# A batched matmul with a decaying running sum: one group of slots by seven block products, and a planner's order in place of a written one

## The chip, the cores and the metric

The kernel runs on one core of a Trainium2 chip. The metric is the device time of one execution in microseconds (us). Before the change the median of three runs is 904.89 us (904.84 to 904.93).

The core's engines work side by side and meet only through semaphores: TensorE (PE) multiplies matrices and writes its results to PSUM; VectorE (DVE), ScalarE (ACT) and GpSimd (POOL) work on tiles; SyncE (SP) issues transfers here. Each engine takes its instructions strictly in the order in which the program issued them, so an instruction that waits holds up all that stand behind it on its engine.

## The reference

```python
# x: 16 x 2048 x 1024, w: 1024 x 1024, decay: 1024, all float32
xw = x @ w
out[:, 0, :] = xw[:, 0, :]
for t in range(1, S):
    out[:, t, :] = decay * out[:, t - 1, :] + xw[:, t, :]
```

One matmul of 32768 x 1024 by 1024 x 1024, and behind it a recurrence over 2048 time steps in each of the 16 x 1024 columns.

## The kernel before

**Tiling.** Time is cut into 64 chunks of 512 steps (four per batch entry). Two neighbouring chunks of one batch entry form a group; the last two chunks are handled singly. The 1024 output columns are eight blocks of 128 (n = 0 to 7), the 1024 inputs eight blocks (k = 0 to 7). A *slot* is one group and one n: 16 matmuls (L131) of 128x128 by 128x512 in bf16, eight for each half of a PSUM tile ps of 128 x 1024. There are three such tiles, used in turn, and single-bank tiles spare and spare1. 31 groups have eight slots each, the last two chunks eight shorter ones each: 264 slots. Slots 112 to 119 are group 14, the first half of a batch entry.

**Input.** `load` (L101) brings a quarter of a chunk into xb (three buffers) by a transfer on POOL's queue that casts to bf16. `turn` (L109) transposes blocks on DVE into xw (two buffers; row L115). `part` (L119) separates the two interleaved bf16 halves on ACT into xt (five buffers; row L123), two instructions for a chunk, named X and Y in the agenda. xt is what the matmuls stream.

**Recurrence.** In a slot's result the columns are on the partitions and time lies along the row, so that a scan on DVE does the recurrence. A tile is either *unpaired*: one full scan over 1024 steps straight from PSUM (`run`, L228); or *paired*: ACT copies ps to xs (`copy`, L185) and scales its even steps by the decay (`odd`, through `decayed`, L170), POOL adds these to the odd steps (`join`, L205), DVE scans the 512 odd steps with the squared decay (`scan`, L210), ACT scales the result (`even`, L170) and POOL adds it to the even steps (`fill`, L253). `zero` (L199, L201) sets the first element of the result tile so, `save` (L257) keeps the last column in keep for the next group of the batch entry. Three of four tiles are paired. Here so has four buffers, xs three, h four.

**Output.** `back` (L265) transposes so on DVE into ot (four buffers). When four slots, a *lump* of 2 MB, are in ot, `Outlet.store` (L289) issues four transfers of 512 KB on SP, one per quarter of the partitions. The first `back` of a later lump that takes the same buffer waits for their landing.

**Order.** What is issued when is written out by hand: `agenda` lists, for the first 34 slots and the last 20, the deeds by letter (p copy, g odd, z zero, j join, S scan, h even, c fill, k save, B back, T turn, X and Y part, L load). In between `usual` makes the same list for each slot, with turns and parts due a fixed number of slots ahead (`later`) and one or two loads per slot. `perform` carries a list out.

Of the kernel before, what the change touches and what calls it, by code (L numbers as in the profile page):

```python
# [2 lines left out]

# [6 lines left out]
FP32 = mybir.dt.float32  # L10
# [15 lines left out]
def kernel(  # L26
# [26 lines left out]
    nc = tc.nc  # L53
# [12 lines left out]
    R = K // 2  # L66
    CH = D // 2
    CR = CH // NQ

    const = ctx.enter_context(tc.tile_pool(name="const", bufs=1))  # L70
    sb = ctx.enter_context(tc.tile_pool(name="sb", bufs=1))
# [20 lines left out]
    wcols = wsb.rearrange("p k (h r) q i -> p k h q r i", h=2)  # L92

    def ot_tile(nj):
        return ring(sb, "ot", 4, [128, nj, CR])

    xb_of = {}
    xw_of = {}
# [19 lines left out]

    def part(c, copy, m0, m1, j0=0, j1=NJ):  # L119
        if c not in xt_of:  # L120
            xt_of[c] = ring(sb, "xt", 5, [128, M, 2, TL], BF16)
        src = xw_of[c][:, m0:m1, j0:j1].rearrange("p m j i e -> p m e (j i)")
        pin(copy(out=xt_of[c][:, m0:m1, :, j0 * P:j1 * P], in_=src))  # L123

# [16 lines left out]
    class Tile:  # L141
# [3 lines left out]
        def __init__(self, g, n, ps, outlets):  # L145
            self.b, self.t0 = chunks[g[0]]
            self.T = TL * len(g)
            self.n, self.ps, self.outlets = n, ps, outlets
            self.paired = n % R != R - 1
            if len(tiles) in flips or len(tiles) - len(slots) in flips:  # L150
                self.paired = not self.paired
            self.turn = len(tiles)
            self.lot = sum(t.paired for t in tiles)
            self.prev = None if self.t0 == 0 else last[n]
            if self.t0 + self.T < S:
                last[n] = const.tile([128, 1], FP32, name=f"keep{n}", bufs=2)
                self.keep = last[n]
            else:
                self.keep = None

        @property
        def so(self):
            if not hasattr(self, "held"):
                self.held = sb.tile([128, 2 * TL + 2], FP32, name=f"so{self.turn % 4}")
            return self.held

        def decayed(self, src, h=None):
            if h is None:
                h = ring(sb, "h", 4, [128, TL])[:, 0:self.T // 2]
            pin(nc.scalar.activation(  # L170
                out=h, in_=src, func=mybir.ActivationFunctionType.Copy,
                scale=dec[:, self.n:self.n + 1]))
            return h
# [5 lines left out]
                self.zero()  # L179
                self.join()  # L180

        def copy(self):
            self.xs = sb.tile([128, 2 * TL], FP32, name=f"xs{self.lot % 3}")[:, 0:self.T]
            for t, ps in self.parts():
                pin(nc.scalar.copy(out=self.xs[:, t:t + ps.shape[1]], in_=ps))  # L185

        def odd(self):
            self.g = ring(sb, "h", 4, [128, TL])[:, 0:self.T // 2]
            for t, ps in self.parts():
                size = ps.shape[1]  # L190
                self.decayed(ps[:, 0:size:2], self.g[:, t // 2:(t + size) // 2])

        def parts(self):
            some = self.ps if isinstance(self.ps, tuple) else (self.ps,)
            return [(i * self.T // len(some), ps) for i, ps in enumerate(some)]

        def zero(self):
            if self.prev is None:
                pin(nc.gpsimd.memset(self.so[:, 1:2], 0.0))  # L199
            else:  # L200
                pin(nc.scalar.copy(out=self.so[:, 1:2], in_=self.prev))  # L201

        def join(self):
            odds = self.xs[:, 1:self.T:2]
            pin(nc.gpsimd.tensor_tensor(out=odds, in0=self.g, in1=odds, op=ALU.add))  # L205

        def scan(self):
            T, n, so = self.T, self.n, self.so
            if self.paired:
                pin(nc.vector.tensor_tensor_scan(  # L210
                    out=so[:, 3:T + 2:2],
                    data0=squares[-1][:, n:n + 1].to_broadcast([128, T // 2]),
                    data1=self.xs[:, 1:T:2],
                    initial=0.0 if self.prev is None else self.prev,
                    op0=ALU.mult,
                    op1=ALU.add,
                ))
            else:
                for t, ps in self.parts():
                    self.run(ps, t, ps.shape[1])  # L220

        def run(self, ps, t, size):
            n, so = self.n, self.so
            if t:
                before = so[:, t + 1:t + 2]
            else:
                before = 0.0 if self.prev is None else self.prev
            pin(nc.vector.tensor_tensor_scan(  # L228
                out=so[:, t + 2:t + 2 + size],
                data0=dec[:, n:n + 1].to_broadcast([128, size]),  # L230
                data1=ps,
                initial=before,
                op0=ALU.mult,
                op1=ALU.add,
            ))
# [5 lines left out]
        def complete(self):  # L241
            if self.paired:
                self.even()
                self.fill()
            if self.keep is not None:
                self.save()

        def even(self):
            self.h = self.decayed(self.so[:, 1:self.T + 1:2])

        def fill(self):
            T = self.T
            pin(nc.gpsimd.tensor_tensor(  # L253
                out=self.so[:, 2:T + 2:2], in0=self.h, in1=self.xs[:, 0:T:2], op=ALU.add))

        def save(self):
            pin(nc.scalar.copy(out=self.keep, in_=self.so[:, self.T + 1:self.T + 2]))  # L257

        def back(self, half=None):
# [13 lines left out]
    class Outlet:  # L273


        def __init__(self, ns, nj, half=0, queues=(nc.sync,), pieces=1):
            self.pieces = pieces
            self.ns, self.missing, self.half = ns, set(ns), half
            self.nj, self.t0, self.queues = nj, half * nj * P, queues
            self.ot = ot_tile(nj)  # L280

        def store(self, b, t0):
            n0 = self.ns[0]
# [132 lines left out]
    def turn_and_load(c):  # L416
# [58 lines left out]
        18: "g16 T7 L h15 j16 p17 g17 B14 z17 c15 X7",  # L475
        19: "S16 j17 p18 B15 L g18 L S17 k16 h16 z18 j18",
        20: "Y7 S19 L c16 k17 h17 T8 k19 L c17",
        21: "p20 g20 L S18 X8 j20 B17 B19",
        22: "L h18 p21 c18 B16 k18 g21 B18 Y8 z20 L j21 S20",
        23: "p22 z21 z22 S21 L h20 g22 T9 c20 h21",  # L480
        24: "k21 k20 j22 S23 X9 L c21 Y9 B20 L",
        25: "B23 k23 p24 B21 g24 z24 j24 S22 z25",
        26: "p25 T10 k22 h22 g25 c22 S24 X10 j25",
        27: "B22 p26 S25 g26 z26 Y10 j26",
        28: "S27 h25 h24 c25 S26 c24",
        29: "B27 h26 c26 T11 p28 g28 j28 B24",
        30: "p29 B25 g29 z28 j29 S28 z29 S29",
        31: "h28 p30 c28 B26 g30 h29 B28 j30 z30",
        32: "c29 S31 S30 h30 B29 c30 p32 g32 z32 j32 B30 B31 L L",
        33: "p33 g33 z33 j33 S32 h32 c32 k32 L L",  # L490
        -20: "z-20",
        -19: "p-20 g-20",
        -18: "j-20 S-19 S-20 k-19 B-19",
# [16 lines left out]
        -1: "S-2 h-4 c-4 a-1 b-1 V",  # L510
    }
    flips = (1, 13, 15, -19, -18, -11, -8, -6, -3, -2)
    later = {}
    begun = {"T": 12, "X": 11, "Y": 11}
    for c in range(5, nch):
        first = c // 2 * K
        ahead = (7, 6, 4) if c % 2 else (11, 10, 8)
        for letter, a in zip("TXY", ahead):
            if c >= begun[letter]:
                later.setdefault(first - a, []).append(f"{letter}{c}")  # L520

    def usual(s):
        paired = [t.paired for t in tiles]
        do = [f"P{s}"] if paired[s] else []
        if paired[s - 1]:
            do.append(f"S{s - 1}")
        if not paired[s]:
            do.append(f"S{s}")
        do.append(f"C{s - 1}")
        if paired[s - 2]:  # L530
            do.append(f"B{s - 2}")
        if not paired[s - 1]:
            do.append(f"B{s - 1}")
        return do + later.get(s, []) + ["L"] * (2 if len(loads) > NQ else 1)

    def rest(s):
        do = [f"S{s - 1}"] if tiles[s - 1].paired else []
        do.append(f"C{s - 1}")
        if tiles[s - 2].paired:
            do.append(f"B{s - 2}")  # L540
        return do + [f"B{s - 1}"] + later.get(s, []) + ["L"] * len(loads)

    def perform(do):
        for deed in do:
            deeds[deed[0]](int(deed[1:] or 0))

    perform(agenda[-99].split())
    spares = [spare] + [ring(psp, "spare1", 1, [128, TL])]
    for step, (g, n) in enumerate(slots):
        T = TL * len(g)  # L550
        left = step - len(slots)
        if n % R == 0:
            ns, nj = range(n, n + R), T // P
            outlets = [Outlet(ns, nj)]
        if left == -R:
            outlets = []
        if step == 0:
# [48 lines left out]
            for k, l in todo:  # L606
                matmul(ps[:, l * TL:(l + 1) * TL], n, k, xt_of[g[l]])
        tiles.append(Tile(g, n, ps, outlets))
        do = agenda.get(step, agenda.get(left) if left >= -20 else None)
        if do is None:  # L610
            do = usual(step)
        else:
            do = do.split()
            if left == -20:
                do = rest(step) + do
        perform(do)
    assert not loads
# [1 line left out]
_INS = ['x', 'w', 'decay']  # L619
# [26 lines left out]
```

## Time and profile before

| what | value |
|---|---|
| median of three runs | 904.89 us |
| the profiled execution | 905.68 us, span 903.9 us, granted clock 0.999 |
| L131, matmuls into ps from xt, 128x512 | x3976, 859.0 us busy |
| L228, full scan of 128x1024 on DVE | 2260 ns, with a carried state 2321 ns |
| L210, paired scan of 128x512 on DVE | 1219 ns, with a carried state 1279 ns |
| L170, scaling of 512 steps on ACT | from so 775 ns, from ps 693 ns |
| DVE waited for L205 (POOL) | 50.9 us, 65 times, longest 1.3 us |
| stores landed, 140 to 200 us / 200 to 400 us (median) | 18.4 us / 11.7 us |
| loads landed, 140 to 200 us / 200 to 400 us (median) | 12.3 us / 7.6 us |

The span is the time between the first and the last event of the profiled execution; the execution's own time is a little longer. Busy times of one engine can overlap slightly at their edges. A row such as "L265 DVE STREAM_TRANSPOSE ot<-so" names the source line, the engine, the operation, and the tiles out and in; behind the bar stand the busy time in all, the mean of one in ns, and the idle time just before them with what ended it.

### The profile page before, as it was taken

Reading aid. Unit: us, or ns where it says so; the run is one execution under the profiler, and the core shown is the slowest. Engines: PE = TensorE matmul, PEld = TensorE weight load, DVE = VectorE, ACT = ScalarE, POOL = GpSimd, SP = SyncE. Lnnn points to the kernel's source line nnn. Section 1 sums busy time; section 2 is a strip of 40 time slices with the busy share of each in tenths; the row PEclk is TensorE's granted clock in tenths of the full one; section 3 lists DMA queues with packets and bytes.
Section 4 is the critical chain, followed back from the end, with each engine's and each line's share of the span. In section 5 each row is a group of like instructions: output and inputs, shape, how many; then the busy total and the mean of one; then the engine's idle time right before and its main releaser. Section 6 shows DMA issues by size and latency. Waiting matters only on the chain.

```text
span 903.9 us, 12113 instructions
## 1 busy us (share of the span) xinstructions
PE 896.4 (99%) x4217; PEld 412.7 (46%) x4217; DVE 825.5 (91%) x628; ACT 686.3 (76%) x957; POOL 656.7 (73%) x755
## 2 busy tenths in 40 slices
PE   8999999999999999999999999999999999999997
PEld 5544444444444444444444444444444444444444
DVE  4999998999999999999998999999999999999997
ACT  4899967777877877877778778778777787787742
POOL 7978678777767768677677677777777776776632
PEclk9999999999999999999999999999999999999999
DMA  9999999999999999999999999999999999999868
GB/s 186 190 215 215 226 256 217 215 237 236 254 242 260 243 251 257 248 237 226 224 237 229 224 229 229 230 224 229 231 227 228 233 232 222 226 233 211 176 143 235
DMA packets 402542, 204.77 MB, mean 227 GB/s; under 512 B 8752, under 2 KB 401456, under 8 KB 402480
## 3 DMA queue, kind: packets, MB, share of 16 engines
q1 hardware_dynamic: 265168, 134.76, 61.0%
q0 software_dynamic: 137024, 68.70, 56.6%
q8 instruction: 33, 0.54, 0.2%
q10 hardware_dynamic: 288, 0.52, 0.2%
q14 instruction: 29, 0.24, 0.1%
HBM read 138.42 MB, written 134.22 MB: 302 GB/s over the span
## 4 chain that ended last, share of the span: by engine, by line
PE 97%; DMA 1%; POOL 0%; issue 0%; DVE 0%; DVEq 0%; POOLq 0%
PE ps L131 96%; DMA xb<-in_x_dram 1%; PE spare L131 1%; POOL xb L105 0%; PE spare L395 0%; PE ps L395 0%; DVE h L399 0%; DVE xw L115 0%; DVEq L115 0%; POOLq L630 0%
## 5 line engine op out<-in xcount | busy, mean ns | idle before, releaser
L131 PE MATMUL ps<-xt,wsb 128*128 128x512 bf16 (+1 forms) x4028 | 866.3, 378 | 0.0
L131 PEld LDWEIGHTS <-wsb 128*128 128x128 bf16 x4168 | 407.5, 98 | 478.0 <-ACT wsb L313 0.8
L205 POOL TENSOR_TENSOR xs<-h,xs 128x512 f32<-128x512 f32 (+1 forms) x190 | 242.8, 1278 | 188.1 <-ACT h L170 85.3
L185 ACT COPY xs<-ps 128x1024 f32<-128x1024 f32 (+1 forms) x190 | 188.9, 994 | 152.9 <-PE ps L131 148.1
L265 DVE STREAM_TRANSPOSE ot<-so 128x1024 f32<-128x1024 f32 (+1 forms) x260 | 300.0, 1191 | 2.1 <-POOL so L199 1.1
L253 POOL TENSOR_TENSOR so<-h,xs 128x512 f32<-128x512 f32 (+1 forms) x190 | 241.0, 1270 | 43.7 <-ACT h L170 27.8
L123 ACT COPY xt<-xw 128x2048 bf16<-128x2048 bf16 (+3 forms) x136 | 242.3, 1790 | 8.7 <-DVE xw L115 8.7
L105 POOL DMA_DIRECT2D xb<-in_x_dram x264 | 174.0, 660 | 5.6 <-DMA xb<-in_x_dram 3.2
L170 ACT ACTIVATE h<-so,dec 128x512 f32<-128x512 f32 (+1 forms) x190 | 145.3, 766 | 28.7 <-DVE so L210 25.2
L115 DVE STREAM_TRANSPOSE xw<-xb 128x2048 f32<-128x2048 f32 (+3 forms) x78 | 147.4, 1901 | 8.0 <-DMA xb<-in_x_dram 7.9
L210 DVE TENSOR_TENSOR_SCAN so<-spare,keep,xs 128x512 f32<-128x512 f32 (+1 forms) x97 | 119.9, 1239 | 26.7 <-POOL xs L205 26.4
L210 DVE TENSOR_TENSOR_SCAN so<-spare,xs 128x512 f32<-128x512 f32 x93 | 113.3, 1219 | 27.4 <-POOL xs L205 24.5
L170 ACT ACTIVATE h<-ps,dec 128x512 f32<-128x512 f32 (+1 forms) x190 | 130.0, 684 | 0.0
L228 DVE TENSOR_TENSOR_SCAN so<-dec,ps 128x1024 f32<-128x1024 f32 x34 | 76.8, 2260 | 1.0 <-ACT h L170 1.0
L228 DVE TENSOR_TENSOR_SCAN so<-dec,keep,ps 128x1024 f32<-128x1024 f32 (+1 forms) x35 | 75.9, 2168 | 0.2 <-issue 0.2
L257 ACT COPY keep<-so 128x1 f32<-128x1 f32 x136 | 25.3, 188 | 9.5 <-DVE so L228 9.0
L201 ACT COPY so<-keep 128x1 f32<-128x1 f32 x97 | 18.4, 191 | 2.7 <-DVE ot L265 2.4
L131 PE MATMUL spare<-xt,wsb 128*128 128x512 bf16 (+3 forms) x60 | 12.6, 329 | 0.0
L131 PE MATMUL ps<-xw,wsb 128*128 128x256 bf16 (+3 forms) x68 | 11.2, 301 | 0.4 <-DVE xw L115 0.4
L199 POOL MEMSET so<- 128x1 f32 x93 | 10.7, 117 | 0.6 <-DVE ot L265 0.6
L331 PE MATMUL spare<-idle 128*128 128x512 bf16 x22 | 6.8, 479 | 1.2 <-DVE idle L321 1.2
L306 POOL DMA_DIRECT2D ot<-in_w_dram x12 | 6.6, 552 | 1.7 <-DMA xb<-in_x_dram 0.8
(39 smaller groups left out, 37.9 us busy)
## 6 DMA issues: line engine op xcount, KB each, us to landing
out_dram<-ot SPq DMA_DIRECT2D x248, 512.0 KB, 10.9
xb<-in_x_dram POOLq DMA_DIRECT2D x248, 256.0 KB, 7.9
out_dram<-ot SPq DMA_DIRECT2D x12, 256.0 KB, 4.2
ot<-in_w_dram POOLq DMA_DIRECT2D x12, 128.0 KB, 5.6
xb<-in_x_dram POOLq DMA_DIRECT2D x8, 128.0 KB, 5.4
out_dram<-xb SPq DMA_DIRECT2D x3, 256.0 KB
xb<-in_x_dram POOLq DMA_DIRECT2D x4, 144.0 KB, 7.0
ot<-in_w_dram ACTq DMA_DIRECT2D x2, 256.0 KB, 5.2
```

The source lines that it names most:

```text
L105: pin(nc.gpsimd.dma_start(out=xb_of[c][quad(q), j0:j1], in_=_ap(x, [[D, P], [P * D, j1 - j0], [1, CQ]], (b * S + t0 + j0 * P) * D + q * CQ)))
L115: pin(nc.vector.transpose(out=dst.rearrange("p (m j i) -> p j m i", m=M, i=P)[:, j0:j1, m0:m1], in_=src.rearrange("p (j m c) -> p j m c", ...
L123: pin(copy(out=xt_of[c][:, m0:m1, :, j0 * P:j1 * P], in_=src))
L131: pin(nc.tensor.matmul(out=ps[:, t0:t1] if ps.shape[1] >= t1 else ps, lhsT=lhs, rhs=rhs, start=(k == 0 and t0 == start), stop=(stop and k ...
L170: pin(nc.scalar.activation(out=h, in_=src, func=mybir.ActivationFunctionType.Copy, scale=dec[:, self.n:self.n + 1]))
L185: pin(nc.scalar.copy(out=self.xs[:, t:t + ps.shape[1]], in_=ps))
L205: pin(nc.gpsimd.tensor_tensor(out=odds, in0=self.g, in1=odds, op=ALU.add))
L210: pin(nc.vector.tensor_tensor_scan(out=so[:, 3:T + 2:2], data0=squares[-1][:, n:n + 1].to_broadcast([128, T // 2]), data1=self.xs[:, 1:T:2 ...
L228: pin(nc.vector.tensor_tensor_scan(out=so[:, t + 2:t + 2 + size], data0=dec[:, n:n + 1].to_broadcast([128, size]), data1=ps, initial=befor ...
L253: pin(nc.gpsimd.tensor_tensor(out=self.so[:, 2:T + 2:2], in0=self.h, in1=self.xs[:, 0:T:2], op=ALU.add))
L257: pin(nc.scalar.copy(out=self.keep, in_=self.so[:, self.T + 1:self.T + 2]))
L265: pin(nc.vector.transpose(out=outlet.ot[:, :, c0:c0 + P], in_=self.so[:, 2 + t0:2 + t0 + nj * P].rearrange("p (i t) -> p i t", t=P)))
```

## The change

The order of slots 34 to 243 is no longer written by hand. `steady` makes a list of jobs, each with an engine, an assumed cost, a key (about when it should start), and the jobs it waits for; `in_order` walks through them in assumed time and gives each engine, whenever it is free, the ready job with the smallest key; the program is then issued in that order. Each engine's start in that walk is `BEGUN`; a load is assumed to land after 11.0 us, a store after 13.0. Loads have a key and an earliest time of their own, evenly spaced. Turns are cut in two halves.

Group 14 (`merged`) computes its 2 x 2 blocks (two halves of the inputs; two chunks as columns; two blocks n of the weights) by seven products of four matmuls each instead of eight. For that, POOL forms 20 differences of weights (`wd`) from about 170 us before the group on, and three sums on DVE and one on POOL combine the group's parts (`sums`; the last is written over xt). The products go to two halves of a ps tile and a spare; partial results are lifted from PSUM by ACT (`lift`) and combined by DVE (`join` in `mixed_pair`). Between a lift or join and the next product in the same bank, PE waits.

Further: the copy of ps goes straight to so (xs is gone; so has seven buffers, ot three, xt four); a lump leaves in 16 transfers of 128 KB (`pieces=4`); which tiles are unpaired is chosen by `SHARE`, by the distance to group 14: none in it, fewer right behind it, a third in the group before, else a quarter. In the agenda of slots 20 to 33 some parts (X8 to Y10) are issued later and loads and last deeds are left to the plan. The names and lines of unchanged deeds stay; L265 becomes L276, L210 L221, L289 L305.

```diff
-            xt_of[c] = ring(sb, "xt", 5, [128, M, 2, TL], BF16)
+            xt_of[c] = ring(sb, "xt", XTS, [128, M, 2, TL], BF16)
...
+    OTS, XTS, SOS, HS = 3, 4, 7, 4
+    FROM, TO = 34, 244
+    SUMS, SUMT = ('dve', 'pool', 'dve', 'dve'), -16
+    WBY, WLEAD, WSTEP = "pool", 170, 4
+    SHARE = {-1: 0.33, 0: 0, 1: 0.12, 2: 0.25, 3: 0.25, 9: 0.25}
+    merged = (14,)
...
         def copy(self):
-            self.xs = sb.tile([128, 2 * TL], FP32, name=f"xs{self.lot % 3}")[:, 0:self.T]
             for t, ps in self.parts():
-                pin(nc.scalar.copy(out=self.xs[:, t:t + ps.shape[1]], in_=ps))
+                pin(nc.scalar.copy(out=self.line[:, t:t + ps.shape[1]], in_=ps))
...
-        def __init__(self, ns, nj, half=0, queues=(nc.sync,), pieces=1):
+        def __init__(self, ns, nj, half=0, queues=(nc.sync,), pieces=4):
...
-        21: "p20 g20 L S18 X8 j20 B17 B19",
-        22: "L h18 p21 c18 B16 k18 g21 B18 Y8 z20 L j21 S20",
+        21: "p20 g20 L S18 j20 B17 B19",
+        22: "L h18 p21 c18 B16 k18 g21 B18 z20 L j21 S20",
...
+    GAP = 0.19
+    BEGUN = {"pe": 0.0, "act": 7.6, "dve": 8.3, "pool": 9.0}
+    LAND = 11.0
+    STORED = 13.0
+    PASS = 0.2158
+    cost = {"p": .91, "g": .6, "z": .12, "j": 1.27, "S": 1.16, "D": 2.2, "h": .68, "c": 1.27,
+            "k": .11, "B": 1.14, "T": 1.14, "X": 1.79, "L": .66, "half": .5, "both": .62,
+            "sum": 2.15, "wpool": 1.15, "wdve": 1.2, "slow": 4.2}
+    each = R * PASS
+    TURN = (0, 3, 4, 5, 6, 8, 9)
+    AHEAD, SPACE = 42, 3.2
+    EXTRA = 18
+    differences = ((1, 0, 1, 1), (1, 1, 0, 0), (0, 0, 0, 1), (0, 1, 1, 1), (1, 0, 0, 0))
...
+            step = (starts.get(c // 2 + 1, at) - at) / (2 * NQ)
+            for q in range(NQ):
+                paced[c, q] = (at - AHEAD - (EXTRA if c // 2 in merged else 0)
+                               + (c % 2 * NQ + q) * step)
...
+            need = starts[c // 2] - 18 + (c % 2) * 8
...
+                ends = [(a, LAND) for a in got]
+                for half in range(2):
+                    turned[c] = Job(
+                        "dve", cost["T"], need + 2 * half,
+                        lambda c=c, h=half: turn(c, 0, NJ, h * M // 2, (h + 1) * M // 2),
+                        ends + [turned.get(c - 1), part_of.get((c - 2, 1)), turned.get(c)])
...
+        def product(out, xs, ws, begin):
+            for k in range(R):
+                pin(nc.tensor.matmul(out=out, lhsT=ws(k), rhs=xs[:, k // 2, k % 2],
+                                     start=begin and k == 0, stop=k == R - 1,
+                                     skip_group_check=True))
...
+                S1, S2, S0 = (sx[0][:, k] for k in range(3))
+                out, one, two = ((S1, b[:, 0:2], b[:, 2:4]), (S2, a[:, 0:2], S1),
+                                 (S0, a[:, 2:4], S2), (b[:, 0:2], a[:, 0:2], b[:, 0:2]))[i]
...
+                "a1": ("a", lambda: S(0), w_at(0, n0), True, TURN[0]),
+                "a2": ("a", lambda: S(1), w_less(1), False, TURN[1]),
+                "b1": ("b", lambda: S(2), w_at(1, n1), True, TURN[2]),
+                "c": ("c", lambda: xb_()[:, 2:4], w_less(4), True, TURN[3]),
+                "a3": ("a", lambda: xa()[:, 0:2], w_less(2), False, TURN[4]),
+                "b2": ("b", lambda: xa()[:, 2:4], w_less(0), False, TURN[5]),
+                "a4": ("a", lambda: xb_()[:, 0:2], w_less(3), False, TURN[6]),
...
+            a1 = mult("a1", done + weights + (after_ps[bank - 3] if bank >= 3 else []))
+            A1 = lift(0, 1, "a", at("a1"), [a1, gone[0]])
+            a2 = mult("a2", [A1])
+            A2 = lift(0, 0, "a", at("a2"), [a2, gone[0]])
+            b1 = mult("b1", [a1])
+            B1 = lift(1, 0, "b", at("b1"), [b1, gone[1]])
+            c = mult("c", [after_spare[0], part_of[c1, 1]])
+            C = join(0, 1, "c", ALU.add, at("c"), [c, A1])
+            after_spare[0] = C
+            a3 = mult("a3", [A2])
+            A3 = join(1, 0, "a", ALU.subtract, at("a3"), [a3, B1])
+            b2 = mult("b2", [B1])
+            B2 = join(0, 0, "b", ALU.subtract, at("b2"), [b2, A2], True)
+            a4 = mult("a4", [A3])
+            A4 = lift(1, 1, "a", at("a4"), [a4, gone[1]])
...
+        order = in_order()
+        for job in order:
+            job.do()
```

## The prediction

> **What bounds the kernel now.** I read the page first, then the chain of waits, the waits of TensorE, the windows of one group of eight slots, the rows by form, and the DMA lists.
>
> The page's busy shares and the first slices:
>
> ```profile
> span 903.9 us, 12113 instructions
> PE 896.4 (99%) x4217; PEld 412.7 (46%) x4217; DVE 825.5 (91%) x628; ACT 686.3 (76%) x957; POOL 656.7 (73%) x755
> PEclk9999999999999999999999999999999999999999
> ```
>
> PE is busy throughout at full granted clock, and DVE is next at 91%. A busy PE need not be the bound, so the chain of waits in order of time (start, length, what) and PE's own waits come next:
>
> ```profile
> 43.64 830.69 PE ps L131 x3848
> ```
>
> ```profile
> PE spare L331 <- DVE idle L321: 1.2, 1, 1.2
> PE spare L331 <- ACT gate L348: 0.7, 1, 0.7
> PE ps L131 <- DVE xw L115: 0.4, 1, 0.4
> ```
>
> For 830.69 us the end is set by 3848 matmuls back to back: 830.69 / 3848 = 0.2159 us each. PE waits 2.3 us in all, and only before 20 us. So the time falls only if PE has fewer matmuls, and it rises by whatever makes PE wait. How much room the others have shows in the windows of the group's stretch. Group 14 is slots 112 to 119. Slot 248, the first of one chunk, begins three half slots (1.73 each) before the piece at 874.33, at 869.15; 136 slots of 16 x 0.2159 = 3.454 earlier is 399.4, where group 14 begins (called t0).
>
> ```profile
> core 0: us, PE busy (x) PEld busy (x) DVE busy (x) ACT busy (x) POOL busy (x), PEclk, DMA share, GB/s
> 399.60:427.20 27.60, 27.60 (x130) 12.48 (x129) 25.52 (x19) 21.49 (x29) 20.97 (x27) 1.00 1.19 229
> ```
>
> In one group of 27.6 us DVE has 2.1 us left, ACT 6.1, POOL 6.6. Added work meets DVE first. The prices, by form:
>
> ```profile
> L265 DVE STREAM_TRANSPOSE ot<-so 128x1024 f32<-128x1024 f32 x248 | 292.4, 1216 | 2.1 <-POOL so L199 1.1 <-POOL so L253 0.4
> L205 POOL TENSOR_TENSOR xs<-h,xs 128x512 f32<-128x512 f32 x183 | 237.6, 1298 | 177.5 <-ACT h L170 79.9 <-issue 53.8 <-ACT so L201 39.1
> L123 ACT COPY xt<-xw 128x2048 bf16<-128x2048 bf16 x124 | 235.7, 1904 | 3.0 <-DVE xw L115 3.0
> L115 DVE STREAM_TRANSPOSE xw<-xb 128x2048 f32<-128x2048 f32 x62 | 141.7, 2285 | 1.7 <-DMA xb<-in_x_dram 1.6
> L185 ACT COPY xs<-ps 128x512 f32<-128x512 f32 x8 | 4.7, 586 | 5.0 <-PE ps L131 5.0
> L123 DVE COPY xt<-xw 128x512 bf16<-128x512 bf16 x2 | 0.8, 382 | 0.0
> L399 DVE COPY xb<-ps 128x512 f32<-128x512 f32 x1 | 0.7, 692 | 0.0
> ```
>
> These are durations; neighbours overlap a little, so from start to start less is paid. DVE's timeline (start, length):
>
> ```profile
> 400.40 2.32 DVE L228 TENSOR_TENSOR_SCAN so<-dec,keep,ps 128x1024 f32<-128x1024 f32 x1
> 402.64 3.47 DVE L265 STREAM_TRANSPOSE ot<-so 128x1024 f32<-128x1024 f32 x3
> 406.06 1.22 DVE L210 TENSOR_TENSOR_SCAN so<-spare,xs 128x512 f32<-128x512 f32 x1
> 407.20 2.28 DVE L115 STREAM_TRANSPOSE xw<-xb 128x2048 f32<-128x2048 f32 x1
> ```
>
> A full scan (L228) takes 402.64 - 400.40 = 2.24, an output transpose (L265) 3.42 / 3 = 1.14, a paired scan (L210) 1.14, or 1.17 with a carried state.
>
> **The matmuls saved.** Group 14 has 8 x 16 = 128 matmuls; four pairs of slots of seven products of four are 112. 16 x 0.2159 = **3.45 us** less on PE, all of it on the bounding chain. Weights and the other groups' matmul counts don't change.
>
> **What the products cost DVE.** Twelve joins (128x512, one operand in PSUM) and three bf16 sums of 128x2048 are new; two full scans become paired ones (2 x (2.24 - 1.15) = 2.2 less). No row shows a join. Below it lies the copy from PSUM, 0.69 (0.61 from start to start); above it the paired scan of the same 512 elements, 1.14. The join reads one element of each operand per step like the copy, and keeps no state, so I take 0.65. A sum lies between the bf16 copy carried on to 2048 elements, at most 4 x 0.38 = 1.5, and the transpose of 2048, 2.29. I take 2.2: it has two inputs to read.
>
> The Trainium skill's "VectorE: DVE Perf Modes", section "The perf-mode tier table", gives about 1.2 us for a bf16 tensor_tensor of 2048 elements. By it the three sums would cost 3.0 us less than I charge, and DVE would reach the group early; no run here shows it yet.
>
> New on DVE is 12 x 0.65 + 3 x 2.2 - 2.2 = 12.2 us, where the group had 2.1 us left and is 3.45 shorter. So the group can't carry it; it is spread. The plan has fewer full scans around (SHARE), runs the sums 16 us ahead, and leaves transposes for later, up to seven so buffers. Whether PE notices is settled by DVE's order in the built program, walked with these prices. Before the group: the full scan of slot 108 can begin at t0 - 10.36 + 0.2 (three slots back, and 0.2 for the hand-over, cautiously: POOL began 0.09 after ACT ended at 404.64); behind it stand one transpose, two sums, a paired scan, a transpose: 2.24 + 1.14 + 4.4 + 1.17 + 1.14 = 10.1, done at t0 - 0.1, just in time for slot 111's full scan.
>
> - From t0: 0.2, slot 111's scan 2.24, transpose 1.14, two paired scans 2.34, two joins 1.3: the first join that a product (a4 of pair 0) waits for ends at 7.2. PE gets there after nine products of 4 x 0.2159, at 7.8.
> - Up to the third pair's first join: five more joins 3.25, three transposes 3.4, three half turns 3 x 1.13, two scans 2.3: 19.5. PE needs it for pair 3's product c after 23 products, at 19.9.
> - Up to pair 3's A3: four joins 2.6, a half turn 1.1, two transposes 2.3, two scans 2.3: 27.8. PE's last product stands behind 132 matmuls, at 28.5.
>
> So DVE is full for 38 us, and arrives 0.4 to 0.7 us ahead each time, of which a hand-over takes 0.2. Every 0.1 us more per join costs about 1 us by the end (11 joins lie on that path). I put a stall of **0.5 us** here. Behind the group no full scan comes before slot 127, so paired tiles, whose banks ACT empties, keep PE free of DVE's backlog.
>
> **ACT and POOL.** ACT lifts 16 halves (16 x 0.59 = 9.4 us) in place of six copies of 1.01, and scales two tiles more. In its order, up to the last lift, stand 16 lifts, four part copies (L123, 1.9), four scalings of the slots around, four more and two saves: 9.4 + 7.6 + 6.2 + 0.4 = 23.6 us of the 28.5. A lift behind a part copy can be up to 1.9 late; the plan places these between lifts that are not due. I take nothing, with 0 to 1.9 as bounds. POOL gets 20 weight differences over 128x512 bf16: at most L205's 1.3 each, 26 us, laid into slots 59 to 83 (83 us), where 6.6 per group are free, 20 in all. So POOL falls up to 6 us behind there; paired scans wait for it, and a full scan queued behind one on DVE must end 6.9 us after its slot. With 2.24 of its own it has 4.5 us of cover, so the bounds are 0 and 1.6; at fewer bytes per element the price is likely under 1.3, and I take 0.
>
> **The other 25 groups.** The list of jobs holds the same work: 24.9 us of DVE by the same prices (2 full scans, 6 paired, 8 output transposes, 4 half turns), of 27.6. The copy now goes into so instead of xs: same row, L185. Loads are issued one per 3.45 us on POOL's queue, at the same 0.66. In slots 21 to 33 the part copies of chunks 8 to 10 move back by one to six slots, because xt has four buffers: in ACT's order chunk 8's waits for slot 23's end, with saves and scalings behind it, and banks not wanted for two slots (6.9 us) cover its 1.9. Nothing.
>
> **Stores.** A lump of 2 MB leaves in 16 issues instead of 4, and each waits for the one eight before it. Issues on SP take:
>
> ```profile
> out_dram<-ot SPq DMA_DIRECT2D x248, 512.0 KB, 10.9
> xb<-in_x_dram POOLq DMA_DIRECT2D x248, 256.0 KB, 7.9
> out_dram<-ot SPq DMA_DIRECT2D x12, 256.0 KB, 4.2
> ```
>
> The shortest issue of L289 is 0.315 us and the median 2.576, for the same size: the long ones wait for room. 16 x 0.315 = 5.0 us is the low end. The high end takes a quarter of the wait each time, 16 x (0.315 + 0.565) = 14.1, against 13.8 us per lump. Even then SP falls back 0.3 us per lump, 15 us in 51 lumps, and a buffer of the ring of three is wanted 27.6 us after its last transpose, which holds 10.9 + 15; behind a waiting issue stand only later stores. So 0. "DMA: Bandwidth & Descriptors" of the Trainium skill, section "Anatomy of one DMA", has about 2 us fixed per transfer; with two transfers in series on each of the eight semaphores that adds 2 us per lump to the landing, which the same cover holds; it speaks against small transfers.
>
> **Sum.** Median 904.89 - 3.45 + 0.5 = 901.9; I say **902.0**. The profiled execution took 905.68 for its span of 903.9, 1.8 around the span and 0.8 over the median; its span should become about 901.
>
> **Rivals.**
> - *A, forecast: hidden as planned.* 901.2 to 903.1. For it: PE waits nowhere now, and each engine has room but in group 14. Chance 0.60.
> - *B, group 14's own waits eat much of it.* A sum has both inputs in SBUF while POOL, 76% busy there, reads too. Should the two exclude each other, each of the three sums waits up to one POOL operation, 1.3, or POOL for the sum: up to 3.9 on a DVE with 0.4 to spare. A lift behind a part copy does the like for 1.9. Half of 3.9, less 0.4, is 1.6: 904.89 - 3.45 + 1.6 + 0.5 = 903.5, from 903.0 to 905. Against: paired scans with a carried state read two SBUF operands and cost only 0.06 more. Chance 0.20, of which 0.04 still faster. "SBUF — State Buffer" of the Trainium skill, section "Who interferes with whom", states this exclusion for two SBUF inputs; no row of this trace has such a pair.
> - *C, slower: a join costs as much as a scan.* At 1.14 the 11 joins on the path bring 11 x 0.49 = 5.4 more, less the 0.7 spare: PE waits 4.7, 904.89 - 3.45 + 4.7 = 906.1. It turns slower than before from 1.03 us per join on. For it: DVE's only two-operand rows here are scans. Against: the copy's 0.69. Chance 0.08.
> - *D, slower: loads come late at the head of DVE's queue.* The last quad of a group's second chunk is issued about 18 us before the group, and its turn is due 10 us before it, in strict order. Before, loads were issued far ahead. Now a landing above some 12.4 us stops DVE at the turn, twice per group, and 0.4 us more each time passes its spare room (2.7): at 12.8, 2 x 1.8 = 3.6, so 0.9 per group, 23 us in 26 groups, 925. For it: between 140 and 200 us loads landed in 12.3 (median). Against: 7.6 from 200 us on, and even spacing should calm it. Chance 0.12.
>
> **Numbers.** Under 0.2% (1.8 us) this kernel's measurement can't be told from no change: faster is below 903.1, slower above 906.7. C's 906.1 lies near that bound, half of it counts as slower. Faster 0.60 + 0.04 = 0.64; same 0.16 + 0.04 = 0.20; slower 0.04 + 0.12 = 0.16. A and B hold 0.80 and span 901.2 to 905, so the range is 901.2 to 905.2.
>
> **What would show it.** PE 16 matmuls fewer and idle about 0.5 us, in the stretch 400 to 430 us, waiting for DVE joins (A: under 1.7; B: 2 to 3, with sums or lifts as releasers; C: joins at 1.1 in the rows). No PE wait elsewhere, DVE's waits on xb near none, store landings under 13 (D: DVE waiting for DMA again and again). PE idle in every group would make the forecast wrong altogether.

## The result and the profile after

The changed kernel takes 919.88 us (median of 4 runs, 917.61 to 920.08) where the kernel before takes 904.91 beside it (904.84 to 904.98): a ratio of 1.016, 95% interval 1.0142 to 1.0177. It is slower by 15 us. The profiled execution took 919.78 us for a span of 918.0, against 903.9 before: 14.1 us to be found.

The page of the changed kernel: span, busy shares, and the shares of the chain that ended last.

```profile
span 918.0 us, 12767 instructions
PE 892.0 (97%) x4120; PEld 411.7 (45%) x4201; DVE 824.8 (90%) x695; ACT 688.3 (75%) x973; POOL 691.7 (75%) x785
PEclk9999999999999999999999999999999999999997
PE 76%; DMA 13%; DVE 3%; issue 2%; ACT 2%; POOL 2%; SPq 1%; DVEq 0%; ACTq 0%; POOLq 0%
```

The saved matmuls are real: 4201 weight loads (PEld), one for each matmul, where there were 4217, 16 fewer. (A trace can lack some records of matmuls themselves, so their own counts say less.) But the span exceeds PE's busy time by 26.0 us where it was 7.5, and a chain that was 97% PE is now 76% PE and 13% DMA. Some 110 us of that chain are stores (12%), in two stretches: from 38.65 to 103.98 us and from 453.44 to 498.5 us. They point at two places; they are no loss of 110 us, since PE works beside them. The chain is followed back from the last work of an engine, so what SP does behind that isn't in it. DVE and ACT are about as busy as before, POOL by 35.0 us more; what is new are waits. From the table of waits, DVE's for a store and PE's behind the first 25 us:

```profile
DVE ot L276 <- DMA out_dram<-ot: 10.0, 2, 5.1
...
PE ps L138 <- DVE so L239: 3.7, 1, 3.7
...
PE ps L138 <- ACT h L184: 1.1, 1, 1.1
...
PE ps L764 <- ACT so L840: 0.7, 2, 0.4
```

The columns are total, times, longest. Two waits of DVE for a store (10.0 us) and four waits of PE: one long, one of 1.1 at 110 us, and two small ones in group 14. They are still less than 14.1 us. The rest is after PE's last matmul. The timelines of SP at the end, first before, then after (start, length, what, count):

```profile
875.98 20.49 SPq L289 DMA_DIRECT2D out_dram<-ot  x14
898.18 1.63 SPq L401 DMA_DIRECT2D out_dram<-xb  x3
899.91 0.67 SPq L401 DMA_DIRECT2D out_dram<-h  x1
```

```profile
879.07 33.55 SPq L305 DMA_DIRECT2D out_dram<-ot  x64
912.72 1.37 SPq L417 DMA_DIRECT2D out_dram<-xb  x3
914.18 0.41 SPq L417 DMA_DIRECT2D out_dram<-h  x1
```

Before, the last stores follow the last copies at once (0.3 us behind DVE's last one). After, DVE's last copy (L415) ends at 903.69, against 899.57 before, 4.1 us late; the stores of these last tiles are issued only at 912.72, because 64 issues of L305 fill SP's queue without a gap from 879.07 to 912.62. So of the 14.1 us, 4.1 were lost while engines worked and the other 10.0 in SP's queue. The 4.1 come out of PE's timeline as -3.45 (the matmuls) + 0.9 (group 14) + 1.1 (at 110) + 3.65 and 1.7 (at 505) = 3.9.

**The stall at 505.** DVE's timeline, with idle time and its releaser in brackets:

```profile
492.18 1.25 DVE L221 TENSOR_TENSOR_SCAN so<-spare,keep,so 128x512 f32<-128x512 f32 x1
498.49 1.25 DVE L276 STREAM_TRANSPOSE ot<-so 128x1024 f32<-128x1024 f32 x1 [5.06 <-DMA out_dram<-ot]
499.65 1.20 DVE L122 STREAM_TRANSPOSE xw<-xb 128x1024 f32<-128x1024 f32 x1
...
503.08 2.30 DVE L239 TENSOR_TENSOR_SCAN so<-dec,keep,ps 128x1024 f32<-128x1024 f32 x1
```

An output transpose stands 5.06 us at the head of DVE's queue for the landing of a store. The full scan behind it, which reads ps itself, ends at 505.38, and PE, which wants that bank, has waited. PE's timeline, and its weight loads right behind the wait:

```profile
505.44 373.07 PE L138 MATMUL ps<-xt,wsb 128*128 128x512 bf16 x1685 [3.65 <-DVE so L239]
```

```profile
505.82 0.15 PEld L138 LDWEIGHTS <-wsb 128*128 128x128 bf16 x1 [0.28 <-issue]
506.24 0.15 PEld L138 LDWEIGHTS <-wsb 128*128 128x128 bf16 x1 [0.28 <-issue]
```

Behind the 3.65 us the next eight loads are 0.43 us apart instead of 0.216: 8 x 0.21 = 1.7 us more. One late store costs 5.3 us of PE.

The late store is that of lump 31, whose buffer lump 34 takes in the ring of three. From the start times of L276 and L305 in the trace: the last transposes of lumps 27 and 28 begin at 412.4 and 432.4, 20 us apart, while group 14's joins fill DVE; those of lumps 28 to 33 follow at 432.4, 444.5, 457.3, 465.3, 479.8 and 489.9, 11.5 us each on the mean instead of 13.8. DVE catches up, and stores don't drain that fast. The sixteen issues of lumps 28, 29, 30 and 31 take 8.1, 10.3, 13.2 and 16.8 us from the first to the last. Lump 31's last transpose ends at 466.5; its issues run from 473.2 to 490.0, behind lump 30's, and the buffer is free at 498.5, 32.0 us later. SP's issues in this stretch (shortest, median and longest in ns, then where they begin):

```profile
L305 SPq DMA_DIRECT2D out_dram<-ot x9: 315/316/316, 479.7 to 488.8; - x9
DMA to landing us min/median/max: 9.4/9.5/9.5
```

An issue takes 0.316 us here, but they begin 1.1 us apart: the ninth of lump 31 at 481.36, just after its first has landed at 481.34, and likewise the next three. SP waits there for the transfer eight before. The windows after and before (busy us and count per engine, clock, DMA share, GB/s):

```profile
455.00:490.00 35.00, 34.84 (x161) 15.87 (x163) 35.00 (x30) 27.64 (x41) 32.56 (x39) 1.00 1.30 237
```

```profile
455.00:490.00 35.00, 35.00 (x164) 15.85 (x163) 32.74 (x24) 26.96 (x37) 25.98 (x32) 1.00 1.20 229
```

In the same 35 us DVE works without a pause, 35.00 us instead of 32.74, and does 13 output transposes instead of 11 (the counts of 30 and 24 also hold turns, which are now in halves). An estimate of what that asks of the transfers: a lump of 2.10 MB each 13.8 us is 152 GB/s, a load of 0.26 MB each 3.45 us another 76, together 228 (229 were measured before). A lump each 11.5 us makes 258, and 237 is what was moved; the best fortieth of the whole span is 252.

**Group 14** itself, by form of the changed kernel (busy, mean ns, idle before):

```profile
L781 DVE TENSOR_TENSOR xt<-xt,xt 128x2048 bf16<-128x2048 bf16 x1 | 2.3, 2312 | 0.0
L781 DVE TENSOR_TENSOR sx<-xt,sx 128x2048 bf16<-128x2048 bf16 x1 | 1.2, 1227 | 0.0
L781 DVE TENSOR_TENSOR sx<-xt 128x2048 bf16<-128x2048 bf16 x1 | 1.2, 1180 | 0.0
L846 DVE TENSOR_TENSOR so<-so,ps 128x512 f32<-128x512 f32 x4 | 2.7, 677 | 0.1
L846 DVE TENSOR_TENSOR so<-so,spare 128x512 f32<-128x512 f32 x4 | 2.6, 652 | 0.0
L623 POOL TENSOR_TENSOR wd<-wsb 128x512 bf16<-128x512 bf16 x20 | 23.2, 1162 | 0.1
```

Joins cost 0.65 to 0.68, sums on DVE 1.2 twice and 2.3 once, weight differences 1.16. PE is idle 0.9 us between 396 and 432 us.

### The profile page after: what moved, and what is told of

Same layout as the page of the kernel before. It is cut to its first block, busy times and chain, and to the rows that moved or that the text cites. A ratio compares the mean times of both kernels' runs of the same rounds, so it can differ in the third digit from the quotient of the medians.

```text
span 918.0 us, 12767 instructions
## 1 busy us (share of the span) xinstructions
PE 892.0 (97%) x4120; PEld 411.7 (45%) x4201; DVE 824.8 (90%) x695; ACT 688.3 (75%) x973; POOL 691.7 (75%) x785
## 4 chain that ended last, share of the span: by engine, by line
PE 76%; DMA 13%; DVE 3%; issue 2%; ACT 2%; POOL 2%; SPq 1%; DVEq 0%; ACTq 0%; POOLq 0%
PE ps L138 74%; DMA out_dram<-ot 12%; DVE ot L276 1%; PE ps L764 1%; POOL xb L112 1%; SPq L305 1%; DVE so L239 1%; DMA xb<-in_x_dram 1%; DVE so L221 1%; ACT h L184 1%; PE spare L138 1%; DMA ot<-in_w_dram 1%; ACT so L840 1%; ACT xt L130 0%; POOL so L216 0%
## 5 line engine op out<-in xcount | busy, mean ns | idle before, releaser
L138 PE MATMUL ps<-xt,wsb 128*128 128x512 bf16 (+1 forms) x3821 | 837.3, 378 | 8.9 <-DVE so L239 3.7
L138 PEld LDWEIGHTS <-wsb 128*128 128x128 bf16 x4040 | 395.2, 98 | 469.2 <-issue 7.7
L264 POOL TENSOR_TENSOR so<-h,so 128x512 f32<-128x512 f32 (+1 forms) x193 | 247.2, 1283 | 122.6 <-ACT h L184 103.5
L276 DVE STREAM_TRANSPOSE ot<-so 128x1024 f32<-128x1024 f32 (+1 forms) x260 | 303.7, 1190 | 35.2 <-POOL so L264 17.9
L216 POOL TENSOR_TENSOR so<-h,so 128x512 f32<-128x512 f32 (+1 forms) x193 | 247.7, 1284 | 75.7 <-ACT h L184 41.3
L202 ACT COPY so<-ps 128x1024 f32<-128x1024 f32 (+1 forms) x185 | 184.0, 995 | 113.6 <-PE ps L138 113.6
L184 ACT ACTIVATE h<-so,dec 128x512 f32<-128x512 f32 (+1 forms) x202 | 154.5, 768 | 25.5 <-DVE so L221 25.0
L122 DVE STREAM_TRANSPOSE xw<-xb 128x1024 f32<-128x1024 f32 (+4 forms) x130 | 153.2, 1190 | 5.3 <-DMA xb<-in_x_dram 5.3
L221 DVE TENSOR_TENSOR_SCAN so<-spare,so 128x512 f32<-128x512 f32 x96 | 113.9, 1196 | 10.0 <-POOL so L216 9.0
L221 DVE TENSOR_TENSOR_SCAN so<-spare,keep,so 128x512 f32<-128x512 f32 (+1 forms) x97 | 117.1, 1213 | 4.0 <-POOL so L216 3.8
L623 POOL TENSOR_TENSOR wd<-wsb 128x512 bf16<-128x512 bf16 x20 | 23.2, 1162 | 0.1
L764 PE MATMUL ps<-xt,wd 128*128 128x512 bf16 x47 | 11.8, 379 | 0.1
```

The lines of the kernel that those rows point to most:

```text
L122: pin(nc.vector.transpose(out=dst.rearrange("p (m j i) -> p j m i", m=M, i=P)[:, j0:j1, m0:m1], in_=src.rearrange("p (j m c) -> p j m c", ...
L138: pin(nc.tensor.matmul(out=ps[:, t0:t1] if ps.shape[1] >= t1 else ps, lhsT=lhs, rhs=rhs, start=(k == 0 and t0 == start), stop=(stop and k ...
L184: pin(nc.scalar.activation(out=h, in_=src, func=mybir.ActivationFunctionType.Copy, scale=dec[:, self.n:self.n + 1]))
L202: pin(nc.scalar.copy(out=self.line[:, t:t + ps.shape[1]], in_=ps))
L221: pin(nc.vector.tensor_tensor_scan(out=so[:, 3:T + 2:2], data0=squares[-1][:, n:n + 1].to_broadcast([128, T // 2]), data1=so[:, 3:T + 2:2] ...
L264: pin(nc.gpsimd.tensor_tensor(out=evens, in0=self.h, in1=evens, op=ALU.add))
```

## The experiments

The first theory was that sixteen transfers per lump cost both losses, at the end and in the middle; its rival, that the stall in the middle belongs to the plan and the ring of three ot buffers, whatever the size of a transfer. Medians below; the kernel before, on the same chip, took 905.02 beside the first four, 905.18 beside the next four, 905.13 beside the last two.

**Four transfers per lump again** (`e1`).

```diff
-        def __init__(self, ns, nj, half=0, queues=(nc.sync,), pieces=4):
+        def __init__(self, ns, nj, half=0, queues=(nc.sync,), pieces=1):
```

> The changed kernel with its lumps stored in 4 transfers of 512 KB instead of 16 of 128 KB, all else kept (ring of three output buffers, plan, group 14 by seven products). Theory S (the sixteen transfers are the whole loss: about 10 us at the end, where the last store issue comes 9 us after the last copy, 5.4 us around 505 us and 1.1 us around 110 us): 919.9 - 10 - 6.5 = 903.4, between 902.5 and 904. Rival R (the two long waits of DVE for stores come from the ring of three buffers, whatever the size of a transfer): the end mends, the waits at 99 and 493 us stay, 909 to 910. Rival M (the products of group 14 themselves and the planner's order cost PE time in other places too): over 905.

Measured 910.99, ratio 1.0067 (1.0052 to 1.0082). The end is mended, 8.9 us less than the changed kernel; the middle isn't. The table of waits of this kernel:

```profile
DVE ot L276 <- DMA out_dram<-ot: 10.4, 3, 6.4
PE ps L138 <- DVE so L239: 6.0, 1, 6.0
```

PE's wait in the middle is even longer, 6.0 against 3.7. The first theory falls for the middle.

**Sixteen, but four in the last twenty slots** (`e2`).

```diff
-        return [Outlet(range(n, n + R), len(g) * NJ)]
+        return [Outlet(range(n, n + R), len(g) * NJ, pieces=1 if step >= TO else 4)]
```

> The changed kernel with 16 transfers in slots 0 to 243 and 4 only in the last 20 slots. Theory S: only the end mends; there 48 to 64 issues of about 0.52 us each are left out of SP's queue, so 919.9 - 10 = 909.9 (909 to 911), with the wait of DVE for stores near 493 us and PE's stall near 505 us as they were. Rival R makes the same of the end. If the end were late for another reason (DVE or POOL late in the last slots), the time would stay within 2 us of 919.9.

Measured 908.63, ratio 1.0031 (1.0019 to 1.0042): this alone takes 11.3 us off. The stall at 505 stays (4.1 us), and 0.7 at 110.

**The kernel before, with sixteen transfers** (`e3`): `pieces=4` in the kernel before, nothing else.

> The kernel before with nothing changed but the transfers: 16 for a lump instead of 4. Theory S: the end is late here too, by about 10 us, as the issues of the last four lumps take 16 x 0.52 = 8.3 us each where a lump of one chunk is made in 6.9: 914.9 (913 to 917). With its ring of four buffers no wait of DVE for a store in the middle. Rival R expects the end alone as well. If the loss needs the planner's order, this kernel stays at 904.9 to 906.

Measured 915.04, ratio 1.011 (1.0095 to 1.0125): 10.0 us slower. Its SP timeline at the end:

```profile
869.63 38.28 SPq L289 DMA_DIRECT2D out_dram<-ot  x66
908.01 1.37 SPq L401 DMA_DIRECT2D out_dram<-xb  x3
```

SP is again without a gap, and the last tiles' stores are 8 us and more behind their copies. PE waits nowhere in the middle; DVE waits 0.3 us in all for stores. So sixteen transfers cost the end 10 us with no product in the kernel, and nothing elsewhere under the old order with its four buffers.

**The plan without the products** (`e4`): `pieces=1` and `merged = ()`; all groups have their 128 matmuls.

> The changed kernel with 4 transfers and with no group by seven products: the planner's order alone, with as many matmuls as before; sums, differences and joins are gone. It bounds what the order itself costs. Theory S: PE waits nowhere, 904.9 to 905.5. Rival M, order half: if the planner's order costs PE time by itself, over 906. The difference to the run with seven products and 4 transfers is what group 14 is worth: 3.45 less its own waits, which the trace of the changed kernel puts at 1.0 to 1.4, so 2.0 to 2.5.

Measured 905.39, ratio 1.0004 (0.9995 to 1.0013). PE has no stall in the middle; DVE waits 3.0 us in all for stores, nearly all of it at 102 us, and PE doesn't see it. Planned order, three ot buffers and evenly spaced loads cost nothing measurable by themselves. The stall needs group 14's products or what the plan does around them: without them `SHARE` makes every fourth tile unpaired throughout, and no run separates the two.

**The stores of the stretch cut in half** (`e6`). Lumps 28 to 31 leave out half of their stores, so that half of that output isn't written; all else is as in `e1`.

```diff
-                for i, q in enumerate((0, 2, 1, 3)):
+                for i, q in enumerate((0, 2) if b == 7 else (0, 2, 1, 3)):
```

> 4 transfers a lump, group 14 by seven products, the changed kernel's own order, and half of the stores of lumps 28 to 31 left out (two quarters of the partitions of batch entry 7 are not written). Theory D: these four lumps drain in half the time, DVE waits for no buffer near 495 us, 911.0 - 7.7 = 903.3. Rival W: unchanged, 910 to 911.

Measured 902.82, ratio 0.9973 (0.9963 to 0.9983). With fewer bytes to drain the stall at 505 is gone, with DVE's order unchanged.

**A ring of four** (`e8`): `e1` with `OTS = 4`. To make room, the weight differences of a pair are all written to one place, so group 14's products use other values than the reference; every engine's instructions are the same.

> 4 transfers a lump, group 14 by seven products, the changed kernel's own order on every engine, and a ring of four output buffers. To make room the five sets of weight differences share one place, so group 14's results are not the reference's; every instruction and its size stays. Theory D, ring part: with four buffers the first transpose of lump 34 waits for lump 30, landed near 484 us, and not for lump 31: no wait of DVE for stores after 480 us, 911.0 - 7.7 = 903.3. Rival W: 910 to 911.

Measured 903.12, ratio 0.9975 (0.9965 to 0.9985). DVE's timeline at the same place:

```profile
494.05 1.25 DVE L221 TENSOR_TENSOR_SCAN so<-spare,keep,so 128x512 f32<-128x512 f32 x1
495.48 1.25 DVE L276 STREAM_TRANSPOSE ot<-so 128x1024 f32<-128x1024 f32 x1 [0.18 <-POOL so L264]
496.64 2.31 DVE L239 TENSOR_TENSOR_SCAN so<-dec,keep,ps 128x1024 f32<-128x1024 f32 x1
```

No transpose waits for a store anywhere, and the full scan begins at 496.64 instead of 503.08. `e6` and `e8` take the stall away from its two sides, the bytes and the buffers; `e4` takes away its origin, group 14 with its plan. Against `e1` this is 7.9 us for one wait of 6.0 and the slow matmuls behind it.

**A plan that knows how stores drain** (`e5`): `pieces=1`, and the plan gets a fifth engine on which lumps drain one after the other.

```diff
+    BEGUN = {"pe": 0.0, "act": 7.6, "dve": 8.3, "pool": 9.0, "sp": 0.0}
...
-                stored[lump] = lumps[lump]
+                drain = Job("sp", 15.5 if 28 <= lump <= 33 else 13.0, key + 9, lambda: None,
+                            [one for one, _ in lumps[lump]])
+                stored[lump] = [(drain, 4.0)]
```

> 4 transfers a lump, group 14 by seven products, ring of three, and a plan that is told how slowly stores drain: in the plan a lump's stores run one lump after the other, 15.5 us for each of lumps 28 to 33 (about what the trace of the changed kernel shows between 458 and 503 us) and 13 elsewhere. Then slot 139's paired scan stands ahead of the first output transpose of lump 34 on DVE. Theory D (DVE stands at the head of its queue before a buffer of ot that the saturated transfers have not emptied, with scans behind it that PE needs): PE's 6.0 us wait near 506 us and the half clock behind it go, 911.0 - 6.0 - 1.7 = 903.3 (902.5 to 904). Rival W (PE waits there for another reason, such as slots 136 to 140's own work being late after group 14): over 907.

Measured 903.21, but from 902.93 to 912.1: nine of twelve executions lie at 902.9 to 903.6, three at 908.0, 911.8 and 912.1; ratio 0.9998 (0.9977 to 1.0019). The stall at 505 is gone. The profile is of one of the long executions:

```profile
DVE ot L276 <- DMA out_dram<-ot: 27.6, 14, 4.8
PE ps L138 <- DVE so L239: 4.0, 1, 4.0
```

Fourteen waits, spread over the run; the longest wait of PE comes of one of them, at 686.92. With three buffers the order holds only while stores land about as usual; what makes them late in some executions the profile of one doesn't tell.

**The same plan with sixteen transfers up to the last twenty slots** (`e7`): `e5` with the edit of `e2`.

> The plan that is told how stores drain, with 16 transfers a lump up to slot 243 and 4 in the last 20 slots. Theory D with size of no matter in the middle: the same as with 4 everywhere, plus the 1.1 us that PE waited near 110 us with 16 transfers in slots before the plan: 903.3 to 904.5. If small transfers drain faster they are a gain here (the run with 4 only in the tail beat the run with 4 everywhere by 2.4 us): under 903.

Measured 903.61, ratio 0.9982 (0.9973 to 0.999), with all eleven executions between 902.67 and 905.09. PE waits 0.7 at 110 and 0.7 in group 14.

**Sixteen in the planned slots only** (`e9`): `pieces=4 if FROM <= step < TO else 1`, to remove the 0.7 at 110.

> The plan that is told how stores drain, 16 transfers a lump in the planned slots 34 to 243 alone, 4 before and after. Theory: the 0.7 us of PE waiting near 110 us goes (DVE's wait for stores there was shorter with 4 transfers and reached PE in none of the runs with 4), so 903.6 - 0.7 = 902.9; PE's waits inside group 14, 1.2 to 1.4, are all that is left over 905.0 - 3.45 = 901.6. Rival: with 4 transfers ahead of the plan the first planned lumps come late and the gain is given back, 903.5 or more.

Measured 903.61, ratio 0.9982 (0.9973 to 0.999): no gain. PE's wait at 110 is indeed gone (the table of waits holds only the two of group 14 behind the first 40 us), and the median is that of `e7`. In the two profiled executions the gain is still there at DVE's last copy, which ends at 896.98 instead of 897.84, and is lost behind it: from there to the end of the span, where only the last stores land, it takes 4.9 us instead of 4.1. Why they take longer, and whether they do in the other executions, is open.

**A ring of four in the given memory** (`e10`): `e1` with four ot buffers, six so buffers instead of seven, and the sums placed in a turn of the ot ring.

```diff
-    OTS, XTS, SOS, HS = 3, 4, 7, 4
+    OTS, XTS, SOS, HS = 4, 4, 6, 4
...
-                    sx[0] = sb.tile([128, 3, 2, 2, TL], BF16, name="sx")
+                    sx[0] = ring(sb, "ot", OTS, [128, 3, 2, 2, TL], BF16)
```

> 4 transfers a lump, the changed plan without the drain times, and a ring of four output buffers with right results: the sums of group 14 lie in one turn of that ring, and six instead of seven result tiles make the rest of the room. The plan itself has 1.6 us of PE waiting in group 14 instead of 0.5. Theory D: no stall near 500 us, 903.0 + 1.1 = 904.1; if the sums' turn in the ring makes DVE wait for stores around 390 us, 905 to 908.

Measured 905.42, ratio 1.0002 (0.9993 to 1.0012). No wait for stores, but in group 14 PE waits 1.3 us for lifts and 0.6, 0.5 and 0.4 for a join, a lift and a part: 2.8 instead of 0.7. So 905.4 lies where the other guess of the expectation had it, but not for its reason. Whether the missing so buffer or the place of the sums brings these was not separated.

The best versions with the whole output are `e7` and `e9`: 1.5 us faster than the kernel before.

## Why the prediction was wrong

**The failed step** is the one headed "Stores", which ended in "So 0", and so did the time: no rival held it. It failed at two places.

*At the end.* The step set a price of 5.0 to 14.1 us of issues per lump against 13.8 us per lump, and let SP fall back at most 15 us because "behind a waiting issue stand only later stores". The price held there: from the first to the last issue of a lump's sixteen are 7.6 to 8.6 us. The period did not. In the last slots, of one chunk each, four slots are 4 x 1.73 = 6.9 us of PE, and the last transposes of the last four lumps end at 879.04, 884.58, 892.06 and 897.42, 6.1 us apart on the mean. SP begins with these lumps 0.0, 2.7, 3.4 and 7.1 us later, and with the last tiles' stores 9.0 us behind DVE's last copy. And at the end of the kernel the later stores are what the end waits for. The step's own low bound had 5.0, its high 14.1, both to be set against 6.9; above 6.9 the end is late. `e3` shows this part alone, +10.0, and `e2` takes it away. (The lines that the step shows under "Issues on SP take" are times from issue to landing; the durations of the issues are the 0.315 and 2.576 us of its text.)

*In the middle.* "A buffer of the ring of three is wanted 27.6 us after its last transpose, which holds 10.9 + 15." Lump 31's was wanted 26.9 us after (466.5 to 493.4), close to that, and took 32.0 to come free. The step used the landing time of an even pace, and its high price didn't hold either: lump 31's issues took 16.8 us, those of 7 of the 65 lumps more than 14.1, because an issue waits for the landing of the one eight before. Once group 14 has held lumps back by 6 us, the following come every 11.5 us, and each stands behind the one before in SP's queue: the delay adds up over four lumps. The prediction asked where DVE's backlog goes and answered that it keeps PE free (paired tiles); it didn't follow the backlog into the stores. `e1` shows that the number of transfers isn't the cause here, `e4`, `e6` and `e8` that group 14 with its plan, the bytes and the ring are, all three together.

The Trainium skill's "Anatomy of one DMA" ("DMA: Bandwidth & Descriptors"), by which the prediction added 2 us per lump, describes the transfers that GpSimd issues; the tail's 64 KB stores, issued by SP, landed in 1.8 us (median, from the issue). At the end it was not this latency but the issuing that cost.

**Matmuls saved, 3.45**: right, by the 16 weight loads. `e6` and `e8`, which have neither of the two losses, lie 2.4 and 2.1 us under the kernel before.

**Group 14, 0.5 us**: too small. PE is idle 0.9 us there, 0.65 of it in two waits for ACT's lifts. Each lift is held up by another ACT copy: the first, 0.30, by the lift before it, the second, 0.35, as in this stretch of the chain that ended last (start, length, what):

```profile
412.35 1.69 ACT xt L130
...
414.56 0.60 ACT so L840
...
415.20 2.76 PE ps L764 x12
```

That second one is the lift behind a part copy, which the forecast costed at nothing, with 0 to 1.9 as bounds, and rival B named. From the medians of `e6` and `e8` the whole loss beside the 3.45 is 1.1 to 1.4 us (905.18 - 3.45 = 901.73, against 902.82 and 903.12); of this 0.2 to 0.5 has no place in the windows.

**Joins at 0.65** were right (0.65 to 0.68), so C falls. **Sums at 2.2** were nearly twice too dear for two of three, 1.18 and 1.23: the row of the Trainium skill ("VectorE: DVE Perf Modes", "The perf-mode tier table", about 1.2) agrees with the trace, and the prediction did worse to go by the transpose. The third took 2.31, and here is rival B's exclusion, in the changed kernel's timelines of DVE and of POOL:

```profile
393.56 1.23 DVE L781 TENSOR_TENSOR sx<-xt,sx 128x2048 bf16<-128x2048 bf16 x1
394.71 2.31 DVE L781 TENSOR_TENSOR xt<-xt,xt 128x2048 bf16<-128x2048 bf16 x1
```

```profile
394.32 1.61 POOL L264 TENSOR_TENSOR so<-h,so 128x512 f32<-128x512 f32 x1
...
396.56 1.62 POOL L216 TENSOR_TENSOR so<-h,so 128x512 f32<-128x512 f32 x1
```

The later sum begins while POOL's operation runs and ends 1.1 us after that one, at 397.02: a sum's own length. POOL's next one starts under the sum and takes 1.62 instead of 1.29, and those that start under the other two sums take 1.80 and 1.61. The Trainium skill's "SBUF — State Buffer", "Who interferes with whom", says this of a DVE instruction with two SBUF inputs and a GpSimd one that reads; this trace agrees. One reserve: the later sum also writes over one of its inputs, the others don't, and no run has it without POOL beside it. What rival B held against the exclusion was no evidence: of keep a paired scan reads one column, not a second stream. The loss is 1.1 us on DVE, once, and PE doesn't see it.

**Loads** landed in 7.4 us (median) and DVE waited 5.3 us for them in all: D falls. **POOL** at nothing was right: PE runs without a wait from 110.09 to 400.33, where the differences lie. **Slots 21 to 33** at nothing were off by 1.1: at 104 us DVE waits 4.9 us for a store, with three ot buffers and sixteen transfers where there were four of each; PE waits 0.7 there in `e2` and `e7`, and in `e1` and `e9`, with four transfers there, not at all.

Of what would show it, "no PE wait elsewhere" failed, and "store landings under 13" held and misled: the median landing is 5.6 us and the longest that the trace tells 10.9, since they count from the issue and not from the end of the transpose.

## What to carry to other kernels

Price a split of transfers in the stretch with the shortest period, which is often the end, as issues on one queue against the time between two lumps; whatever is last in that queue is the end of the kernel. When work is postponed to make room for a peak, follow it through to the stores: a catch-up fills buffers faster than the mean, and a ring that holds at the mean pace may not hold then. Count a buffer's time from the last write to the landing, the wait in the issuing queue included, not from the issue.

## What the hardware showed unasked

- Where nothing else holds them, issues of stores on SP come about half a microsecond apart: the last lump's sixteen, of 64 KB, begin 0.507 us apart (904.6 to 912.2, 15 steps), those of lump 61, of 128 KB, 0.508. The shortest, 0.315, is not what a row of them pays. They don't wait for the one eight before, which lands 1.8 us after its issue, while eight issues take 4. Where transfers land late they do: lump 31's begin 1.1 us apart, with 8 to 9.5 us to landing.
- Behind PE's wait of 3.65 us eight matmuls ran 0.43 us apart, behind 6.0 us in `e1` twelve; the granted clock is 0.93 in the window from 490 to 515 us and 0.64 from 506 to 510. Behind the 1.1 us at 110 there is none of it (matmuls begin 0.215 us apart). "TensorE: Matmul & The Clock Gate" of the Trainium skill, "Part 1: The HAM clock gate", has half rate after a window of about 3.4 us without work; these three cases agree.
- With one plan and one ring of three, executions lie 9 us apart with four transfers per lump (`e5`) and 2.4 or 0.8 us with sixteen in the planned slots (`e7`, `e9`). Why was not settled.
